# A hybrid encoder layer on one NeuronCore: side tasks placed by shared PSUM banks, a later hand-over of key tiles, a reordered last period and scan

## The chip, the core and the metric

The kernel runs on one core of one Trainium2 chip. The metric is the device time of one execution in microseconds (us). Engines are named as in the profile: PE is TensorE (PEld its weight loads), DVE is VectorE, ACT is ScalarE, POOL is GpSimd, SP is SyncE, which here issues the DMAs. Each engine runs its own instructions in order and waits on semaphores of the others.

## What is computed

One layer over 2048 tokens of 1024 features, all in float32:

```
hn   = rms_norm(h) ;  proj = hn @ w_in           # 4 head groups' q, k, v, gates; z; xbc; dt; memory q, gate
att  = window_attention(rotary(q), rotary(k), v, sink) * silu(g_attn)    # |q-k| <= 128, 16 heads, 4 key heads
xbc  = silu(depthwise_conv5(xbc))
y    = ssd_scan(forward) + ssd_scan(backward) + d_skip * xs              # chunks of 128, states of 128 x 64
ssd  = group_rmsnorm(y * silu(z))
xat  = softmax(q_mem . mk) . mv * silu(g_mem)    # 4 heads, 256 memory tokens
out  = rms_norm(h + concat[att, ssd, xat] @ w_out)
```

## The kernel before

Products that need accuracy are made of three float32r products each: operands are split into a high part (an ACT cast, line 174) and a low part (a DVE subtraction, line 175), and `split3` multiplies high by high, high by low and low by high. These projections write PSUM tiles named `pj`, of which there are three banks. All side work shares the five others: two banks `s` (scores, states), two banks `t` (transposes, sums), one bank `o` (outputs).

After a start that prepares the memory keys and values, the tokens are worked off in four periods of 512, c = 3, 2, 1, 0, from the last to the first. A period computes keys and values, then for each of four head groups g the heads' queries and gates (`heads`), convolution inputs (`conv`), `z_gate` and `mem_project`. In period 0 all eight `conv` stand ahead of the groups. Then `early` multiplies the finished attention and memory columns of the late blocks by half of w_out, and `out_block` does the rest for each of 16 blocks of 128 tokens.

Beside this main stream run side tasks, written as generators: window attention of one block (`attention`), `mem_attention`, the local part of the SSD (`ssd_local`), the decay sums (`steps`), and at the end the forward scan (`incoming` and `forward`, one block after the other). A task runs until a `yield`, whose number says after how many microseconds it may go on. That time is counted on `clock`, a plan of TensorE's work that `mm` and `tr` advance for every matmul written. `main` lets the due tasks write their next piece after every few projection matmuls. So the plan fixes TensorE's order. The other engines' orders come from the framework's scheduler, which works with its own estimates.

A piece is written when its own time has come. Whether the bank that it will write has been read out is not asked: TensorE then waits at that matmul, and everything behind it in TensorE's order waits too. In `attention` block 0 of a group loads the keys and values (`khh`, `kll`, `vg`) and waits 9.0. The three other blocks go on when the tiles stand in `kv`:

```
            kv["t"] = kst, vg
            yield 9.0
        yield from take("pm", 4)
        while "t" not in kv:
            yield 0.5
```

Queries go through `rope`, are stored to `q_d` and loaded again as `qs`, transposed in HBM (lines 472 and 473). `rope` uses the tiles `rt0` and `rt1`, one buffer each. In the scan, `forward` of one block loads `yy` from `y_d` (line 731), adds `inc` (736), multiplies by z (738), squares on ACT (739), adds on DVE (741), sums on TensorE (`t<-ones,b`), makes a factor, spreads it on TensorE (`t<-yo,ones`), multiplies four times (line 756) and stores to `mix_d` (758). `yy` has one buffer, so the load for the next block waits for that store.

Of the kernel before, what the change touches and what calls it, by code (L numbers as in the profile page):

```python
# [45 lines left out]
def layer(ctx: ExitStack, tc: tile.TileContext, a: dict):  # L46
# [38 lines left out]

    def bank(pl, name):
        return pl.tile([P, 512], F32, name=name)

# [120 lines left out]
    def rope(pa, pb, tab):  # L209

        n = tab.shape[-1]
        t, u = (misc.tile([P, 2, CH], F32, name=f"rt{i}")[:, :, :n] for i in range(2))
# [3 lines left out]
        hi = as32r(misc.tile([P, 2, CH], F32, name="rt1")[:, :, :n])  # L216
        split(hi, as32r(t), t)
        return hi, as32r(t)
# [161 lines left out]
    def steps(s, nb, raw):  # L380
# [21 lines left out]
        yield 18.0  # L402
        pf = bank(ps_t, "t")
# [5 lines left out]
        mm(pf[:, 256:256 + n], ones, raw.rearrange("p b r -> p (b r)"), True, True)  # L409
        fl = fc.rearrange("p b d r -> p (b d r)")  # L410
# [6 lines left out]
        yield 1.5  # L417
        pt = bank(ps_t, "t")
        nc.tensor.transpose(pt[:n, :P], fl, ident)
# [61 lines left out]
    def attention(c, g, i, qs, gt, kv):  # L481
# [7 lines left out]
        if i == 4 * c:  # L489
# [35 lines left out]
        yield 14.0 if c or g < 3 else 9.0  # L525
# [3 lines left out]
        for n_, j in enumerate(order):  # L529
            if n_ == 2:  # L530
                yield 0.7
            tt = bank(ps_t, "t")
            for r in range(4):
                tr(tt[:, r * P:(r + 1) * P], pm[:, r, j * P:(j + 1) * P])
            if n_ == 1:
# [4 lines left out]
        held["pm"] += 4  # L540
        oo = bank(ps_o, "o")
        for j in order:
            vv = vg[:, k0 + j - lo]
            mm(oo[0:64, 0:256], vv, pts[j][:, 0:256], j == order[0], j == order[-1])
            mm(oo[64:128, 0:256], vv, pts[j][:, 256:512], j == order[0], j == order[-1])
        held["pt"] += nk
# [32 lines left out]
    def ssd_local(blocks):  # L579
# [4 lines left out]
        for i, (c, g) in enumerate(parts):  # L584
# [4 lines left out]
            xc, ee = nxt  # L589
            tt = bank(ps_t, "t")  # L590
            for j in range(3):
                tr(tt[:, j * P:(j + 1) * P], xc[:, j])
            nat = sp.tile([P, 3 * P], F32, name="nat", bufs=1)
            nc.scalar.copy(nat, tt[:, :3 * P])  # L594
            pc = bank(ps_s, "s")
            mm(pc[:, :P], xc[:, 2], xc[:, 3], True, True)
            cbm = sp.tile([P, 2, P], F32, name="cbm")
# [14 lines left out]
            yield 14.0  # L612
            py = bank(ps_o, "o")
            for pr in range(2):
                for u in range(2):
                    r = 2 * pr + u
                    mm(py[u * 64:(u + 1) * 64, pr * P:(pr + 1) * P], nat[:, r * 64:(r + 1) * 64], gg[:, r], True, True)
            yo = sp.tile([P, 2, P], F32, name="yo")
# [3 lines left out]
            nc.sync.dma_start(y_d[2 * g:2 * g + 2, :, c * P:(c + 1) * P].rearrange("j p t -> p j t"), yo)  # L622
            pst = bank(ps_s, "s")
            mm(pst, nat[:, 256:384], xd.rearrange("p d r e -> p (d r e)"), True, True)
            so = sp.tile([P, 2, 256], F32, name="carry")
# [7 lines left out]
    def mem_project(c, xs, hd):  # L633
# [12 lines left out]
        return spawn("mem", mem_attention(c, hd, qh, ql, gm, mkt))  # L646

    def mem_attention(c, hd, qh, ql, gm, mkt):
        yield 11.0
        pms = []  # L650
        for half in range(2):
            ss = bank(ps_s, "s")
            for j in range(2):
                tl = slice((2 * half + j) * P, (2 * half + j + 1) * P)
                for _ in split3(ss[:, j * MEM:(j + 1) * MEM], [(qh[:, tl], ql[:, tl], mkt[:, :MEM], mkt[:, MEM:])]):
                    pass
            mx = misc.tile([P, 2], F32, name="mmx", bufs=3)
# [11 lines left out]
            if half:  # L669
                mvt = mkt.rearrange("p (u m d) -> p u m d", u=2, m=2)  # L670
                nc.sync.dma_start(as32(mvt), mv_d[:, :, :, hd * P:(hd + 1) * P].rearrange("u m p d -> p u m d"))
            yield 2.0 if half == 0 else 10.0
        yield from take("pt", 2)
        pts = []
        for m in range(2):
            tt = bank(ps_t, "t")
            for q in range(4):
                tr(tt[:, q * P:(q + 1) * P], pms[q // 2][:, q % 2, m * P:(m + 1) * P])
            hi = ap_.tile([P, 512], F32R, name="pt", bufs=3)
# [6 lines left out]
        yield 2.0  # L686
        oo = bank(ps_o, "o")
        for _ in split3(oo, [(mvt[:, 0, m], mvt[:, 1, m], pts[m][1], pts[m][2]) for m in range(2)]):
            pass
        held["pt"] += 2  # L690
# [3 lines left out]
    def incoming(c):  # L694
# [13 lines left out]
        yield 5.0  # L708
        for d, st_ in enumerate((state["f"], hbt)):
            py = bank(ps_s, "s")  # L710
            for pr in range(4):
                mm(py[:, pr * P:(pr + 1) * P], st_[:, pr * P:(pr + 1) * P], cc[:, pr // 2], True, True)
            nc.vector.tensor_tensor(ef[:, d], py.rearrange("p (q t) -> p q t", q=4), ef[:, d], ALU.mult)
            if d == 0:
                yield 1.0
# [7 lines left out]
    def forward(c):  # L723
# [18 lines left out]
        yield 15.0  # L742
        pn = bank(ps_t, "t")
        for g in range(2):
            mm(pn[:, g:g + 1], zv[:, g, 0], ones[:, 0:1], True, True)
        rn = sp.tile([P, 2], F32, name="rn", bufs=2)
# [118 lines left out]
    nz = [0] * NPER  # L865
    for c in range(NPER - 1, -1, -1):
# [3 lines left out]
        if c == 0:  # L870
            for i in range(8):
                main(conv(c, xs, i))
# [218 lines left out]
```

## Time and profile before

| | us |
|---|---|
| Median of three runs (lowest and highest) | 1881.1 (1878.04 to 1883.53) |
| The profiled execution | 1886.97 |
| its span, from first to last instruction | 1885.3 |
| PE busy in the span | 1770.2 |
| DVE busy, ACT busy, POOL busy | 1183.9, 925.1, 263.9 |

The profile shows one execution. Busy time of PE is a modelled one, since matmuls are pipelined. Idle time in front of an instruction stands in brackets in the timeline, with what ended it. PEclk is the granted clock of TensorE: 1.00 is 2.4 GHz and 0.50 is 1.2 GHz.

### The profile page before, as it was taken

What the parts mean: (1) busy time and instruction counts of PE and PEld (TensorE: products, weight loads), DVE (VectorE), ACT (ScalarE), POOL (GpSimd) and SP (SyncE); (2) the same over time, 40 slices, a digit from 0 to 9 for tenths busy, and PEclk for the clock granted to TensorE, in tenths of its full rate; (3) what the DMA queues carried; (4) which work ended last, traced back from release to release, by engine and by line L of the source; (5) the groups of instructions that cost most, each with busy time, mean ns of one, the idle gap of its engine ahead of it and who ended that gap; (6) DMA issues with size and microseconds to landing.
All of it is one profiled execution on the core that took longest, in us unless ns stands there. A gap on an engine that the chain in (4) does not pass through costs nothing.

```text
span 1885.3 us, 26616 instructions
## 1 busy us (share of the span) xinstructions
PE 1770.2 (94%) x9242; PEld 1441.6 (76%) x9242; DVE 1183.9 (63%) x2669; ACT 925.1 (49%) x1985; POOL 263.9 (14%) x253
## 2 busy tenths in 40 slices
PE   6789999998999999989999998999898989999998
PEld 6777878876778777866778787777676778888876
DVE  7456666686666668767576679866777543344332
ACT  6246546563756457456556665465566421111111
POOL 0000000012110000211000012211122233333220
PEclk9899999999999999999999999999999999999999
DMA  6746374577664755766474566655667765555442
GB/s 233 220 147 203 110 236 130 153 231 234 212 183 136 222 157 163 246 196 206 135 209 142 166 199 204 219 171 155 204 176 207 244 168 168 169 173 160 136 140 79
DMA packets 262695, 341.31 MB, mean 181 GB/s; under 512 B 29344, under 2 KB 171808, under 8 KB 262560
## 3 DMA queue, kind: packets, MB, share of 16 engines
q1 hardware_dynamic: 262560, 339.61, 59.2%
q8 instruction: 73, 1.20, 0.3%
q14 instruction: 62, 0.51, 0.1%
HBM read 251.20 MB, written 88.34 MB: 180 GB/s over the span
## 4 chain that ended last, share of the span: by engine, by line
PE 67%; DMA 14%; DVE 11%; ACT 4%; issue 3%; POOL 1%; SPq 1%; DVEq 0%; POOLq 0%; ACTq 0%
PE pj L156 50%; PE s L156 7%; PE o L156 5%; PE t L160 4%; DMA qs<-q_d 3%; DVE wl L175 2%; DMA q_d<-rt 2%; DMA cu<-in_x_dram 1%; DMA fb<-ef_d 1%; ACT wh L174 1%; DMA ws<-in_w_in_dram 1%; DMA mxl<-mix_d 1%; PE t L156 1%; DMA mix_d<-b 1%; DVE pm L512 1%
## 5 line engine op out<-in xcount | busy, mean ns | idle before, releaser
L156 PE MATMUL pj<-xh,wh 128*128 128x512 f32 (+2 forms) x1296 | 507.5, 392 | 1.6 <-ACT msq L852 1.6
L156 PE MATMUL pj<-xl,wh 128*128 128x512 f32 (+2 forms) x1296 | 495.9, 383 | 1.9 <-DVE xl L175 1.9
L156 PE MATMUL pj<-xh,wl 128*128 128x512 f32 (+2 forms) x1296 | 495.4, 382 | 0.1
L156 PEld LDWEIGHTS pj<-xh,wl 128*128 128x128 f32 x1296 | 247.5, 191 | 46.1 <-DVE wl L175 1.0
L156 PEld LDWEIGHTS pj<-xh,wh 128*128 128x128 f32 x1296 | 247.9, 191 | 40.9 <-issue 4.8
L156 PEld LDWEIGHTS pj<-xl,wh 128*128 128x128 f32 x1296 | 248.0, 191 | 36.8 <-DVE xl L175 2.4
L175 DVE TENSOR_TENSOR wl<-ws,wh 128x1024 fp32r<-128x1024 f32 (+2 forms) x175 | 211.4, 1209 | 96.1 <-ACT wh L174 89.5
L174 ACT CAST wh<-ws 128x1024 fp32r<-128x1024 f32 (+2 forms) x175 | 179.8, 1028 | 139.5 <-PE pj L156 96.9
L512 DVE CUSTOM_DVE_ANT_0 pm<-s,band,sink 128x384 f32<-128x384 f32 (+1 forms) x256 | 148.9, 594 | 68.6 <-PE s L156 66.9
L520 ACT ACTIVATE pm<-pm,mx 128x385 f32<-128x385 f32 (+1 forms) x256 | 151.2, 594 | 64.4 <-DVE mx L518 64.2
L608 POOL TENSOR_TENSOR b<-nat,win 128x256 f32<-128x256 f32 x64 | 44.3, 711 | 912.9 <-ACT nat L594 912.9
L156 PE MATMUL pj<-woh,mxh 128*128 128x512 f32 x416 | 171.4, 412 | 0.0
L156 PE MATMUL pj<-wol,mxh 128*128 128x512 f32 x416 | 166.1, 399 | 0.0
L156 PE MATMUL pj<-woh,mxl 128*128 128x512 f32 x416 | 166.1, 399 | 0.0
L156 PE MATMUL s<-khh,qs 128*128 128x384 f32 (+1 forms) x256 | 97.2, 380 | 55.0 <-DMA qs<-q_d 28.7
L524 ACT ACTIVATE pm<-pm,den 128x384 f32<-128x384 f32 (+1 forms) x256 | 132.9, 593 | 14.7 <-DVE den L522 14.7
L174 ACT CAST mxh<-mxl 128x512 fp32r<-128x512 f32 x64 | 39.6, 619 | 198.4 <-DMA mxl<-mix_d 94.9
L538 ACT COPY pt<-t 128x512 f32<-128x512 f32 x120 | 69.8, 582 | 103.7 <-PE t L160 103.5
L156 PEld LDWEIGHTS s<-khh,qs 128*128 128x128 f32 x256 | 50.3, 196 | 82.6 <-issue 35.1
L452 DVE SCALAR_TENSOR_TENSOR cu<-raw,cw,cu 128x512 f32<-128x512 f32 (+2 forms) x128 | 98.7, 778 | 15.6 <-ACT cu L450 14.5
L175 DVE TENSOR_TENSOR mxl<-mxl,mxh 128x512 fp32r<-128x512 f32 x64 | 50.4, 788 | 89.9 <-ACT mxh L174 89.8
L160 PE MATMUL t<-ident,pm 128*128 128x128 f32 x736 | 101.1, 274 | 2.7 <-ACT pt L538 1.8
(217 smaller groups left out, 2948.1 us busy)
## 6 DMA issues: line engine op xcount, KB each, us to landing
ws<-in_w_in_dram SPq DMA_DIRECT2D x152, 512.0 KB, 4.2
q_d<-rt SPq DMA_DIRECT2D x32, 512.0 KB, 5.5
qs<-q_d SPq DMA_DIRECT2D x32, 512.0 KB, 6.3
fb<-f_d SPq DMA_DIRECT2D x32, 512.0 KB, 4.6
mxl<-mix_d SPq DMA_DIRECT2D x64, 256.0 KB, 3.8
mix_d<-ao SPq DMA_DIRECT2D x64, 128.0 KB, 3.7
xc<-xbc_d SPq DMA_DIRECT2D x32, 256.0 KB, 3.8
st_d<-carry SPq DMA_DIRECT2D x32, 256.0 KB, 4.0
```

The lines of the kernel that those rows point to most:

```text
L156: nc.tensor.matmul(out, lhsT=lhsT, rhs=rhs, start=start, stop=stop)
L160: nc.tensor.transpose(out, in_, ident)
L174: nc.scalar.copy(hi, x)
L175: (eng or nc.vector).tensor_tensor(lo, x, as32(hi), ALU.subtract)
L452: nc.vector.scalar_tensor_tensor(u, raw[:, r0 + k:r0 + k + cnt], cw[:, i, k:k + 1], u, ALU.mult, ALU.add)
L512: nc.vector.tensor_tensor_reduce(pm[:, r, :w], ss[:, :w], band[:, ms], 1.0, sink8[:, 4 * g + r:4 * g + r + 1], ALU.add, ALU.max, mx[:, r:r ...
L520: nc.scalar.activation(pm[:, r, :w + 1], pm[:, r, :w + 1], AF.Exp, bias=mx[:, r:r + 1], scale=0.125, accum_out=den[:, r:r + 1])
L524: nc.scalar.activation(pm[:, r, :w], pm[:, r, :w], AF.Copy, scale=den[:, r:r + 1])
L538: nc.scalar.copy(pts[j], tt)
L608: nc.gpsimd.tensor_tensor(xd[:, d], nat[:, 0:256].rearrange("p (r e) -> p r e", r=4), win[:, d, 4 * g:4 * g + 4].unsqueeze(2).broadcast_to ...
```

## The change

Five edits. (1) `bank` notes for the shared banks until when each is taken, `slot` makes a task wait until the next bank of its kind is free by the plan's clock, and `reads` sets that time behind the last matmul into it: now plus 1.0 to 3.0. Every side task calls them, and some fixed waits change. (2) The key tiles are handed over after the wait, which is 10 instead of 9. (3) `mvt`, the memory values, has a tile of its own and is loaded by `mem_project`, not into the keys' tile later. (4) `rope` uses the four `xp` buffers where its pieces are small. (5) The last period spreads `conv` and `z_gate` over its groups, the waits of the scan are shorter and longer in places, and `early` may go on until the scan's second block is done.

```diff
+    turn = {"s": 0, "t": 0, "o": 0}
+    until = {"s": [0.0] * 2, "t": [0.0] * 2, "o": [0.0]}
+
     def bank(pl, name):
+        if name in turn:
+            until[name][turn[name] % len(until[name])] = clock[0] + 3.0
+            turn[name] += 1
         return pl.tile([P, 512], F32, name=name)
+
+    def slot(name, n=1):
+        while True:
+            u = until[name]
+            t = max(u[(turn[name] + i) % len(u)] for i in range(n))
+            if t <= clock[0]:
+                return
+            yield max(t - clock[0], 0.1)
+
+    def reads(name, us, back=1):
+        u = until[name]
+        u[(turn[name] - back) % len(u)] = clock[0] + us
...
     def rope(pa, pb, tab):
+        small = 2 * n <= XW
+        def half(name):
+            if small:
+                return misc.tile([P, XW], F32, name="xp", bufs=4)[:, :2 * n].rearrange("p (j t) -> p j t", j=2)
+            return misc.tile([P, 2, CH], F32, name=name)[:, :, :n]
...
     def attention(c, g, i, qs, gt, kv):
+            yield 10.0
             kv["t"] = kst, vg
-            yield 9.0
         yield from take("pm", 4)
...
         for r in range(4):
+            yield from slot("s")
             ss = bank(ps_s, "s")
             mm(ss[:, :w], qs[:, r, tl], kst[0][:, ks], True, False)
             mm(ss[:, :w], qs[:, r, tl], kst[1][:, ks], False, True)
+            reads("s", 1.7)
...
-                yield 1.2
+                yield 0.6
...
-        yield 14.0 if c or g < 3 else 9.0
+        yield 14.0 if c else 10.0
...
     def mem_project(c, xs, hd):
-        return spawn("mem", mem_attention(c, hd, qh, ql, gm, mkt))
+        mvt = misc.tile([P, 2, 2, P], F32R, name="mvt")
+        nc.sync.dma_start(as32(mvt), mv_d[:, :, :, hd * P:(hd + 1) * P].rearrange("u m p d -> p u m d"))
+        return spawn("mem", mem_attention(c, hd, qh, ql, gm, mkt, mvt))
...
     def incoming(c):
-        yield 5.0
+        yield 7.0
         for d, st_ in enumerate((state["f"], hbt)):
+            yield from slot("s")
             py = bank(ps_s, "s")
...
             if d == 0:
-                yield 1.0
+                yield 0.6
...
     def forward(c):
-        yield 15.0
+        yield 11.0
+        yield from slot("t")
         pn = bank(ps_t, "t")
...
-        yield 4.0
+        yield 5.5
+        yield from slot("t")
         pn = bank(ps_t, "t")
         mm(pn[:, :2 * P], ones, dg.rearrange("p g t -> p (g t)"), True, True)
+        reads("t", 2.0)
...
-        if c == 0:
-            for i in range(8):
-                main(conv(c, xs, i))
-            ssd_t = spawn("ssd", ssd_local(range(3, -1, -1)))
...
-            if c == 0 and g < 3:
+            if c == 0:
                 need(mem_t)
                 mem_t = main(mem_project(c, xs, g))
...
+            for i in range(2 * g, 2 * g + 2) if c else ((0, 1, 2, 3, 4), (5, 6, 7), (), ())[g]:
+                main(conv(c, xs, i))
+                if i == 7:
+                    ssd_t = spawn("ssd", ssd_local(range(4 * c + 3, 4 * c - 1, -1)))
+            for i in (g,) if c else ((), (0,), (1,), (2, 3))[g]:
+                main(z_gate(c, xs, i))
...
     rest_wo()
+    while last > 3 and not fwd[1].done:
+        main(early(last))
+        last -= 1
     for c in range(NB):
         main(out_block(c))
```

The matmuls are the same 8479 instructions in another order. On PE in the last period, where the first two blocks of head group 3 are written (`khh`, `kll`: keys, high and low; `qs`: queries; `mkt`: memory keys), there stood before:

```order
L156 MATMUL s<-khh,qs 128x256
L156 MATMUL s<-kll,qs 128x256
L156 MATMUL s<-khh,qs 128x256
L156 MATMUL s<-kll,qs 128x256
L156 MATMUL s<-mkt,qh 128x256 x2
L156 MATMUL s<-mkt,ql 128x256
L156 MATMUL s<-mkt,qh 128x256 x2
L156 MATMUL s<-mkt,ql 128x256
L156 MATMUL s<-khh,qs 128x256
L156 MATMUL s<-kll,qs 128x256
```

and for the same head group now, with projections in between:

```order
L177 MATMUL s<-khh,qs 128x256
L177 MATMUL s<-kll,qs 128x256
L177 MATMUL pj<-xh,wh 128x512
L177 MATMUL pj<-xl,wh 128x512
L177 MATMUL pj<-xh,wl 128x512
L177 MATMUL pj<-xh,wh 128x512
L177 MATMUL pj<-xl,wh 128x512
L177 MATMUL pj<-xh,wl 128x512
L177 MATMUL s<-khh,qs 128x256
L177 MATMUL s<-kll,qs 128x256
```

Four tiles that share two banks followed each other at once; now six projection matmuls stand between two of them.

On PE in the scan, around the sum `t<-ones,b` of one block (`s<-cbm`: what comes in from the states for the next block; `pj`: output products), before:

```order
L156 MATMUL pj<-woh_14708,mxl 128x512
L156 MATMUL pj<-woh_14714,mxh 128x512
L156 MATMUL pj<-wol_14713,mxh 128x512
L156 MATMUL pj<-woh_14714,mxl 128x512
L156 MATMUL t<-ones,b_15295 128x1 x2
L156 MATMUL pj<-woh_14319,mxh 128x512
L156 MATMUL pj<-wol_14318,mxh 128x512
```

and after:

```order
L177 MATMUL s<-cbm,state 128x128 x4
L177 MATMUL pj<-woh_14096,mxh 128x512
L177 MATMUL pj<-wol_14095,mxh 128x512
L177 MATMUL pj<-woh_14096,mxl 128x512
L177 MATMUL pj<-woh_14725,mxh 128x512
L177 MATMUL pj<-wol_14724,mxh 128x512
L177 MATMUL pj<-woh_14725,mxl 128x512
L177 MATMUL s<-cbm,b_15581 128x128 x4
L177 MATMUL t<-ones,b_15567 128x1 x2
```

The sum moved up to right behind the products with the states. From one block's `t<-yo,ones` to the next block's `t<-ones,b` there stood 66 `pj` matmuls, and 48 stand there now; from `t<-ones,b` to `t<-yo,ones` 24, and now 30.

On DVE at the first keys (`rt` or `xp`: rope; `wl`: low part of a weight), before:

```order
L175 TENSOR_TENSOR rt_629<-rt_629,rt_634 128x2x320
L507 COPY pm<-sink_133 128x4 x2
L175 TENSOR_TENSOR wl<-ws,wh 128x544
L214 TENSOR_TENSOR rt_667<-pj,tab 128x2x320
L213 TENSOR_TENSOR rt_666<-pj,tab 128x2x320
L215 TENSOR_TENSOR rt_666<-rt_666,rt_667 128x2x320
```

and after:

```order
L539 COPY pm<-sink_133 128x4 x2
L196 TENSOR_TENSOR xp<-xp 128x640
L241 TENSOR_TENSOR xp<-pj,tab 128x640
L242 TENSOR_TENSOR xp<-pj,tab 128x640
L196 TENSOR_TENSOR wl<-ws,wh 128x544
L243 TENSOR_TENSOR xp<-xp 128x640
```

The low part of the last value weights moved behind the two rope products that read PSUM.

## Rows read from the trace of the kernel before

**Rows 1.** The page's busy times: engine, busy us (share), instructions.

```profile
PE 1770.2 (94%) x9242; PEld 1441.6 (76%) x9242; DVE 1183.9 (63%) x2669; ACT 925.1 (49%) x1985; POOL 263.9 (14%) x253
```

**Rows 2.** Waits of PE, whole span: line, releaser, total us, times, longest.

```profile
PE s L156 <- DMA qs<-q_d: 28.7, 7, 7.5
PE s L156 <- DVE mx L512: 24.6, 17, 3.5
...
PE t L156 <- DVE b L741: 6.0, 1, 6.0
```

**Rows 3.** Busy times by stretch: stretch, length, PE PEld DVE ACT POOL, PEclk, DMA, GB/s.

```profile
110.00:1075.00 965.00, 918.14 (x4894) 743.06 (x4893) 650.46 (x1491) 562.50 (x1229) 67.93 (x68) 0.98 0.59 181
1075.00:1470.00 395.00, 366.68 (x2001) 294.38 (x2000) 302.08 (x737) 235.08 (x523) 78.49 (x71) 0.97 0.64 196
1470.00:1886.00 416.00, 399.18 (x1876) 327.71 (x1874) 164.48 (x331) 81.48 (x160) 110.21 (x100) 0.98 0.53 155
```

**Rows 4.** The same view, four stretches right behind waits for queries.

```profile
118.58:122.45 3.87, 3.87 (x14) 3.79 (x15) 1.65 (x6) 0.00 (x0) 0.00 (x0) 0.50 0.01 3
...
463.38:467.19 3.81, 3.81 (x10) 3.33 (x11) 1.25 (x4) 0.00 (x0) 0.00 (x0) 0.50 0.73 250
...
815.79:818.77 2.98, 2.98 (x8) 2.69 (x9) 1.25 (x4) 0.00 (x0) 0.00 (x0) 0.50 0.77 263
549.12:552.53 3.41, 3.41 (x14) 1.82 (x15) 0.19 (x2) 0.00 (x0) 0.24 (x1) 0.50 0.47 133
```

**Rows 5.** Timeline of PE, period 2's first scores: start, us, instruction, [idle before].

```profile
455.23 0.39 PE L156 MATMUL pj<-xl,wh 128*128 128x512 f32 x1
455.46 0.39 PE L156 MATMUL pj<-xh,wl 128*128 128x512 f32 x1
463.38 0.66 PE L156 MATMUL s<-khh,qs 128*128 128x384 f32 x1 [7.54 <-DMA qs<-q_d]
```

**Rows 6.** Timeline of PE and DVE around one wait for a score bank.

```profile
861.82 0.34 PE L156 MATMUL s<-khh,qs 128*128 128x384 f32 x1
...
863.88 2.15 DVE L575 SCALAR_TENSOR_TENSOR b<-fb,fc,b 128x128 f32<-128x128 f32 x3
...
867.21 0.69 PE L156 MATMUL s<-khh,qs 128*128 128x384 f32 x1 [3.48 <-DVE mx L512]
```

**Rows 7.** Timeline of all engines, one block of the scan.

```profile
1579.56 0.60 PE L156 MATMUL t<-yo,ones 128*128 128x256 f32 x2
...
1581.35 0.36 SPq L758 DMA_DIRECT2D mix_d<-b  x1
...
1583.66 0.38 SPq L731 DMA_DIRECT2D b<-y_d  x1
...
1586.62 1.28 POOL L736 TENSOR_TENSOR b<-b,fb 128x512 f32<-128x512 f32 x1 [5.72 <-DMA b<-y_d]
...
1590.30 0.58 DVE L741 TENSOR_TENSOR b<-b 128x256 f32<-128x256 f32 x1 [1.85 <-ACT b L739]
...
1597.09 0.50 PE L156 MATMUL t<-ones,b 128*128 128x1 f32 x4
```

**Rows 8.** The same, first, second and last of the scan's 15 links.

```profile
1476.26 0.59 PE L156 MATMUL t<-yo,ones 128*128 128x256 f32 x2
...
1492.99 0.41 DVE L741 TENSOR_TENSOR b<-b 128x256 f32<-128x256 f32 x1
...
1500.66 0.59 PE L156 MATMUL t<-yo,ones 128*128 128x256 f32 x2
...
1523.86 0.41 DVE L741 TENSOR_TENSOR b<-b 128x256 f32<-128x256 f32 x1
...
1819.39 0.67 PE L156 MATMUL t<-yo,ones 128*128 128x256 f32 x2
...
1832.09 0.42 DVE L741 TENSOR_TENSOR b<-b 128x256 f32<-128x256 f32 x1 [4.31 <-ACT b L739]
```

**Rows 9.** Timeline of DVE and PE at the first keys' rope.

```profile
66.56 0.72 DVE L175 TENSOR_TENSOR wl<-ws,wh 128x544 fp32r<-128x544 f32 x1
...
72.73 0.82 DVE L214 TENSOR_TENSOR rt<-pj,tab 128x640 f32<-128x640 f32 x1 [5.44 <-DMA k_d<-rt]
...
73.70 0.57 PE L156 MATMUL pj<-wh,xh 128*128 128x272 f32 x1 [5.25 <-DVE rt L214]
```

More of the change, by code (lines that the diff above doesn't have):

```diff
@@ L211, in rope @@
         n = tab.shape[-1]
-        t, u = (misc.tile([P, 2, CH], F32, name=f"rt{i}")[:, :, :n] for i in range(2))
+        small = 2 * n <= XW
[3 more added lines that the diff above has]
+            return misc.tile([P, 2, CH], F32, name=name)[:, :, :n]
+        t, u = half("rt0"), half("rt1")
         nc.vector.tensor_tensor(t, pa.unsqueeze(1).broadcast_to([P, 2, n]), tab[:, 1:3], ALU.mult)
@@ L215, in rope @@
         nc.vector.tensor_tensor(t, t, u, ALU.add)
-        hi = as32r(misc.tile([P, 2, CH], F32, name="rt1")[:, :, :n])
+        hi = as32r(half("rt1"))
         split(hi, as32r(t), t)
@@ L409, in steps @@
         mm(pf[:, 256:256 + n], ones, raw.rearrange("p b r -> p (b r)"), True, True)
+        reads("t", 1.6)
         fl = fc.rearrange("p b d r -> p (b d r)")
@@ L529, in attention @@
         for n_, j in enumerate(order):
-            if n_ == 2:
-                yield 0.7
+            yield from slot("t")
             tt = bank(ps_t, "t")
@@ L534, in attention @@
                 tr(tt[:, r * P:(r + 1) * P], pm[:, r, j * P:(j + 1) * P])
+            reads("t", 1.3)
             if n_ == 1:
@@ L540, in attention @@
         held["pm"] += 4
+        yield from slot("o")
         oo = bank(ps_o, "o")
@@ L545, in attention @@
             mm(oo[64:128, 0:256], vv, pts[j][:, 256:512], j == order[0], j == order[-1])
+        reads("o", 1.4)
         held["pt"] += nk
@@ L589, in ssd_local @@
             xc, ee = nxt
+            yield from slot("t")
             tt = bank(ps_t, "t")
@@ L612, in ssd_local @@
             yield 14.0
+            yield from slot("o")
             py = bank(ps_o, "o")
@@ L622, in ssd_local @@
             nc.sync.dma_start(y_d[2 * g:2 * g + 2, :, c * P:(c + 1) * P].rearrange("j p t -> p j t"), yo)
+            yield from slot("s")
             pst = bank(ps_s, "s")
             mm(pst, nat[:, 256:384], xd.rearrange("p d r e -> p (d r e)"), True, True)
+            reads("s", 1.4)
             so = sp.tile([P, 2, 256], F32, name="carry")
@@ L651, in mem_attention @@
         for half in range(2):
+            yield from slot("s")
             ss = bank(ps_s, "s")
@@ L656, in mem_attention @@
                     pass
+            reads("s", 3.0)
             mx = misc.tile([P, 2], F32, name="mmx", bufs=3)
@@ L674, in mem_attention @@
         pts = []
+        yield from slot("t", 2)
         for m in range(2):
@@ L685, in mem_attention @@
             pts[m] = tt, hi, lo
-        yield 2.0
+        yield 3.0
+        yield from slot("o")
         oo = bank(ps_o, "o")
@@ L689, in mem_attention @@
             pass
+        reads("o", 1.4)
         held["pt"] += 2
@@ L741, in forward @@
         nc.vector.tensor_tensor(zv[:, :, 0], zv[:, :, 0], zv[:, :, 1], ALU.add)
-        yield 15.0
+        yield 11.0
+        yield from slot("t")
         pn = bank(ps_t, "t")
@@ L745, in forward @@
             mm(pn[:, g:g + 1], zv[:, g, 0], ones[:, 0:1], True, True)
+        reads("t", 1.0)
         rn = sp.tile([P, 2], F32, name="rn", bufs=2)
@@ L889, in layer @@
                 norm_x(c - 1, rows_x(c - 1, dg))
-            if c:
-                main(conv(c, xs, 2 * g))
-                main(conv(c, xs, 2 * g + 1))
-                if g == 3:
-                    spawn("ssd", ssd_local(range(4 * c + 3, 4 * c - 1, -1)))
-            for _ in range(1 if c else ((1, 1, 1, 0))[g]):
-                main(z_gate(c, xs, nz[c]))
-                nz[c] += 1
+            for i in range(2 * g, 2 * g + 2) if c else ((0, 1, 2, 3, 4), (5, 6, 7), (), ())[g]:
[4 more added lines that the diff above has]
+                main(z_gate(c, xs, i))
             if c:
@@ L902, in layer @@
         if c == 0:
-            need(mem_t)
-            mem_t = main(mem_project(c, xs, 3))
-            for i in range(nz[c], NG):
-                main(z_gate(c, xs, i))
             fwd = [spawn("fwd", forward(b)) for b in range(NB)]
```

18 lines of the change are left out of this document (11 added, 7 removed).

## The prediction, made before the changed kernel was run

> **What bounds the kernel now.** First the busy times: PE is busy for 1770.2 of 1885.3 us, the next engine for 63% [rows 1]. The change moves matmuls and adds none, so the 1770 can only shrink where the clock was low; what can be won is PE's idle time and what a low clock costs behind it. Second, the waits of PE [rows 2]: 28.7 us in seven waits for the queries `qs`, 24.6 us in 17 waits for a score bank that DVE (line 512) has not read out, then single ones, of which the scan's 6.0 (line 741) matters here. Third, the stretches [rows 3]: PE idles 965 - 918.1 = 46.9 us in the periods 3 to 1, 28.3 in the last period with the attention that follows it, 16.8 in the scan and output stage. The first 110 us are a start that the change touches at one place only. Fourth, the clock: behind waits for queries PEclk reads 0.50, which is 1.2 GHz, in four stretches of 3.0 to 3.9 us [rows 4], though PE is busy there from end to end. A wait so costs more than its length.
>
> Matmuls of 512 columns follow each other at 0.23 us [rows 5]. With this and the like spacing of the smaller forms I count distances along both orders, as us of matmul work at full clock.
>
> **Queries due (edit 2).** In the old order the hand-over stood ahead of the wait of 9, so only block 0 waited; the blocks behind it wrote their scores at once. From the last matmul of the query projection to the first score stood 21.3 us of work in period 2, and PE still waited 7.54 us there [rows 5], so the queries took 28.8. Over the 16 groups the shortest distance was 17.7; it is 29.2 now, 30.8 at the place just named. Only one short wait, in the last period, meets a distance that hardly grew (34.9 before, 36.7 now). I let all 28.7 go; at most 3 come back. What the clock loses behind them goes too: half of 3.87 + 3.81 + 2.98 + 3.41 = 14.1 us, since busy time at 1.2 instead of 2.4 GHz counts double, so 7.0 [rows 4]. Term one: -36 (bounds -30 and -36). What comes late next? The attention of a group starts some ten us later, and its transposes and outputs with it; they have the next group's projections as cover, since the plan has work to put between until the end of the last period.
>
> **Bank read-outs (edit 1, and with it 3 and the last period of 5).** What is left of idle time between 110 and 1470 us is 46.9 + 28.3 - 28.7 = 46.5 [rows 2, 3]. The low clock costs (1 - 0.98) x 965 + (1 - 0.97) x 395 = 31 us there by the stretches' rounded clock [rows 3]; without the 7.0 of term one, and without the low clock that only met idle time, I put it at 20, an estimate. So 66 us are at stake. Which of it goes? Counted along the order, a shared bank (s, t, o) was taken again with under 1.5 us of matmul work behind its last matmul at 52 places, mostly in the last period; now at 17. Waits at such places go. But a wait like the one at 867 stays possible: the bank's matmul ran at 861.82, and its reader stood in DVE's queue behind 2.15 us of SSD work (line 575) and more, so the bank came free 5 us later [rows 6]. The note of 1.7 us knows nothing of that queue. I take 60% of the last period's share (28.3 idle and 9 of clock, -22) and a quarter of the other 30 (-8). Term two: -30, bounds 0 and -55.
>
> A rule of the Trainium skill speaks against it. Rows first: the score waits repeat all through, 17 of them, 24.6 us [rows 2]. "Perfetto Trace Analysis", section Identifying Performance Opportunities, says that the same gap repeating on the engine that should be saturated can mean that there isn't enough PSUM for the next tile, so a matter of buffer count. The change adds no bank. By that rule term two would be nothing; it is the first rival below. That the waits sat at close places in the order speaks for respacing, the queue at 867 for the rule.
>
> The early load of `mvt` puts one DMA at another place in SP's queue. It waits for the previous head's products, as the load of the keys beside it does already, so it adds no new block there. Cost nothing; if its cover failed, the weight loads behind it on SP would be late by the same wait, under 3 us a time, 16 times.
>
> **The start (edit 4).** DVE waited 5.44 us for the keys' store before line 214, and PE 5.25 behind it [rows 9]. That wait can go, since `xp` has four buffers. But the low part of the value weights (0.72 us), which ran at 66.56, now stands behind both rope products, and PE needs it for six matmuls before it reaches the place of the old wait. So the wait for the table of angles holds PE one step earlier. I take 0, bounds -4 and +2.
>
> **The scan (rest of edit 5).** Each block's chain is: `t<-yo,ones`, four products, a store to `mix_d`, the load of the next `yy` into the same buffer, two POOL operations, a square, line 741, then `t<-ones,b`. In the block shown, `t<-yo,ones` starts at 1579.56, the store is issued at 1581.35, the load at 1583.66, POOL starts at 1586.62, line 741 ends at 1590.88: 11.3 us. PE came to `t<-ones,b` at 1597.09, 17.5 us behind [rows 7], so 6 us of slack. Now 48 matmuls stand there, not 66: 17.5 - 18 x 0.23 = 13.4 us. Read the same way, the 15 links take 17.1 (the first), 23.6 (the second, which waits 6.0 today) to 13.1 (the last) [rows 2, 8], 14.4 on average, and eight lie above 13.4, by 26 us in sum. If nothing else changed, the stage would wait 26 instead of 6, and some low clock on top: +32 at most. But in four of the long ones line 741 stood in DVE's order behind two products (line 713) that waited for a DMA; in the new order those stand behind line 741, for they follow from matmuls right ahead of the sum. That takes some 3 us off each. I take +9, bounds -8 and +32. The other half of the loop grows from 24 to 30 matmuls, 1.4 us more for the factor, which is cover. At the end the last block's output begins 42 matmuls, 9.7 us, behind its last `t<-yo,ones`; store and load took 7 us in the block shown [rows 7] and the split follows: 0, bounds 0 and +3.
>
> **Sum.** Against the profiled execution, 1887.0 (its span and 1.7 around it): -36 - 30 + 0 + 9 = -57, so 1830. That execution lay 5.9 above the median of three runs, so 1824 on their scale.
>
> **Rivals.**
> The bank waits move and do not go. For it: DVE's queue [rows 6], and that the number of banks is the same. Against it: 52 close places and now 17. Then only terms one and the scan count: 1881.1 - 36 + 9 = 1854. Chance 0.20.
>
> The scan becomes the bound, slower than before. PE has to wait at each of the 15 sums, and each wait of 3 us and more drops the clock, which costs another 1.7 (half of the 3.41 us seen at 0.50 [rows 4]). It decides once it eats 66 us, 4.4 a link, that is from links of 13.4 + 2.7 = 16 us on average. Today they are 14.4, with links of 17.1 and 23.6 as witnesses, and the denser order puts more DMA traffic into each us. With 18.5 us: 5.1 + 1.7 = 6.8 a link, 102 in all, so 1881.1 - 66 + 102 - 6 = 1911. Against it: the plain chain is 11.3. Chance 0.08.
>
> The spacing does not do what it says: the plan's clock runs away from the chip, because TensorE's work takes longer than it books, and each respaced tile meets other queues on DVE. New waits as long as the old ones then eat term two and half of term one: 1881.1 - 18 + 15 = 1878. For it: DVE's and ACT's orders come from other estimates than the plan's. Against it: a plan that runs late only adds distance. Chance 0.07.
>
> All of the bank waits and the scan's go: 1881.1 - 36 - 55 - 8 = 1782. Chance 0.05.
>
> **The numbers.** My forecast, 1824, has 0.60, with its own range 1804 to 1848. The first rival widens the range to 1868, the good end to 1797. Three tenths of a per cent, 5.6 us, is about what a measurement of this kernel tells from no change. Faster than that: the forecast, the first rival, the good case and a little of the third, 0.86. Within: most of the third, 0.06. Slower: 0.08.
>
> **What would show it.** In the profile after: no row of waits for `qs` above 3 us in sum, and PEclk 1.00 where the four stretches stood; waits on line 512's successor around 15 us with longest ones of 2 to 4 us behind SSD work on DVE; in the last period's stretch idle time near 14 us; waits of `t<-ones,b` in the scan 10 to 20 us in sum, in short pieces. I am wrong in the main step if the score waits keep their 24 us, wrong in the scan's if they are gone or above 35.

## The result and the profile after

The changed kernel takes 1849.8 us (median of four runs, 1848.8 to 1855.0), 0.985 of the time before (0.982 to 0.988). The forecast, 1824, was 57 below the median of before; measured are some 28 by the ratio, 31 between the medians. The sign held, and the whole range (1797 to 1868) holds the result; the forecast's own range (1804 to 1848) just misses it, and the size is half of what was forecast. Profiled: 1848.8, span 1847.1, so 38.2 below the profiled execution of before, which lay high.

The page's busy times answer to [rows 1]:

```profile
PE 1755.7 (95%) x9242; PEld 1426.0 (77%) x9242; DVE 1179.9 (64%) x2681; ACT 921.4 (50%) x1985; POOL 260.3 (14%) x253
```

Waits of PE in the changed kernel (line, releaser, total us, times, longest), to be read against [rows 2]:

```profile
PE s L177 <- DVE mx L546: 14.7, 13, 6.8
...
PE pj L177 <- ACT mxh L195: 8.9, 1, 8.9
PE t L177 <- DVE b L792: 8.1, 7, 2.0
PE t L181 <- ACT nat L632: 6.7, 4, 4.7
...
PE s L177 <- ACT carry L670: 3.8, 1, 3.8
...
PE t L181 <- ACT pm L558: 2.4, 3, 1.1
```

No row for `qs` is left of 28.7 us. The score banks fell from 24.6 to 14.7. New are `mxh` (the high part of a block's finished columns), `nat` (transposed SSD inputs), `carry` (SSD states) and `pm` (softmax weights), 21.8 us together: casts, copies and scalings on ACT that PE hardly waited for before. The stretches, as in [rows 3]:

```profile
110.00:1075.00 965.00, 929.11 (x4986) 749.45 (x4986) 666.63 (x1522) 572.65 (x1251) 70.65 (x70) 0.99 0.61 186
1075.00:1470.00 395.00, 375.95 (x2046) 299.51 (x2045) 282.30 (x717) 231.52 (x520) 58.06 (x59) 0.98 0.63 194
1470.00:1848.00 378.00, 360.30 (x1709) 296.33 (x1707) 160.83 (x324) 68.97 (x138) 122.20 (x109) 0.99 0.60 177
```

PE idles 35.9 us in the first stretch (46.9 before), 19.0 in the second (28.3), 17.7 in the third (16.8). Over the span idle time fell from 115.1 to 91.4, and PE's busy time by 14.5.

Where do the new waits come from? The timeline of the changed kernel at three of them (start, us, engine, instruction, [idle before it]):

```profile
118.78 0.34 PE L177 MATMUL s<-khh,qs 128*128 128x384 f32 x1
...
122.73 1.28 ACT L610 ACTIVATE b<-fb,fc 128x128 f32<-128x128 f32 x4 [6.24 <-DMA fb<-f_d]
123.17 1.23 DVE L611 SCALAR_TENSOR_TENSOR b<-fb,fc,b 128x128 f32<-128x128 f32 x4 [5.74 <-ACT b L610]
...
127.49 0.61 DVE L546 CUSTOM_DVE_ANT_0 pm<-s,band,sink 128x384 f32<-128x384 f32 x1
...
128.17 0.69 PE L177 MATMUL s<-khh,qs 128*128 128x384 f32 x1 [6.76 <-DVE mx L546]
...
467.87 0.63 ACT L302 ACTIVATE cu<-cu 128x512 f32<-128x512 f32 x1 [8.29 <-DMA cu<-in_x_dram]
...
468.50 0.57 ACT L670 COPY carry<-s 128x512 f32<-128x512 f32 x1
...
469.11 0.69 PE L177 MATMUL s<-khh,qs 128*128 128x384 f32 x1 [3.82 <-ACT carry L670]
...
1394.14 0.38 PE L177 MATMUL s<-xc 128*128 128x128 f32 x2
...
1402.71 1.30 ACT L195 CAST mxh<-mxl 128x512 fp32r<-128x512 f32 x2 [7.69 <-DMA mxl<-mix_d]
1403.38 0.79 PE L177 MATMUL pj<-wh,mxh 128*128 128x512 f32 x1 [8.86 <-ACT mxh L195]
```

At 128 the score of 118.78 is read at 127.49, since DVE stood before an SSD operation (line 611) which needs a load through ACT. At 469 the bank's copy stood on ACT behind a square (line 302) which waited 8.3 us for a load of `x`. At 1403 the first `early` block's own columns arrive late. All three end at an operation on DVE or ACT that stands behind a DMA: the first two are late readers of a bank, the third makes an operand. Two stand within 10 us of where the waits for queries at 118 and 463 stood.

### The profile page after: what moved, and what is told of

Same layout as the page of the kernel before. It is cut to its first block, busy times and chain, and to the rows that moved or that the text cites. A ratio compares the mean times of both kernels' runs of the same rounds, so it can differ in the third digit from the quotient of the medians.

```text
span 1847.1 us, 26627 instructions
## 1 busy us (share of the span) xinstructions
PE 1755.7 (95%) x9242; PEld 1426.0 (77%) x9242; DVE 1179.9 (64%) x2681; ACT 921.4 (50%) x1985; POOL 260.3 (14%) x253
## 5 line engine op out<-in xcount | busy, mean ns | idle before, releaser
L177 PEld LDWEIGHTS pj<-xh,wl 128*128 128x128 f32 x1296 | 246.0, 190 | 46.9 <-DVE wl L196 2.7
L195 ACT CAST mxh<-mxl 128x512 fp32r<-128x512 f32 x64 | 39.5, 617 | 162.8 <-DMA mxl<-mix_d 105.7
L181 PEld LDWEIGHTS t<-ident,pm 128*128 128x128 f32 x736 | 86.5, 142 | 34.6 <-ACT nat L632 7.6
L177 PE MATMUL o<-pt,vg 128*64 128x256 f32 x736 | 93.8, 388 | 1.6 <-DVE dq L425 0.7
```

Source lines behind the costliest of these rows:

```text
L177: nc.tensor.matmul(out, lhsT=lhsT, rhs=rhs, start=start, stop=stop)
L181: nc.tensor.transpose(out, in_, ident)
L195: nc.scalar.copy(hi, x)
```

## The experiments

All ratios are against the kernel before on the same chip, with their 95% interval; the changed kernel's is 0.985.

**One edit alone, and all but one.** `e1_handover` is the kernel before with edit 2, `e7_banks` before with edits 1 and 3, `e8_bank_hand` before with all three. `e2_noslot` and `e6_oldhand` are the changed kernel without edit 1, and without edit 2.

```diff
# e1, in the kernel before; e6 is the reverse, in the changed kernel
+            yield 10.0
             kv["t"] = kst, vg
-            yield 9.0
# e2, with the fixed waits of before put back
     def slot(name, n=1):
-        while True:
+        return
+        yield
```

> The kernel before with edit 2 alone (the key tiles are handed over after a wait of 10). The forecast's term one as it stands: all seven waits for queries (28.7 us) and 7.0 of low clock go, 0.981 of before, 1845. Theory after the traces, that a wait removed on TensorE comes back in part as a wait for a bank whose reader is queued behind other work: in the changed kernel 6.8 us stand at 128 and 3.8 at 469, near where 6.9 and 7.5 stood; so some 20 to 24 of the 36 remain, 0.988, 1858. In the profile: no row for queries, the row of score banks longer than the 24.6 us of before.

> The changed kernel with `slot` returning at once and the fixed waits of before between scores, transposes and outputs (1.2, 0.7, 2.0, 1.5, 1.0): edit 1 alone undone. Forecast's term two: most of 30 us come back, 1875, waits for score banks near 24 us again. Theory that the spacing won next to nothing because the waits moved into the queues of the reading engines: within 8 us of the changed kernel, 1842 to 1858, and the total idle time of TensorE within 10 us of the changed kernel's 91.

> The changed kernel with edit 2 undone: the key tiles are handed over ahead of the wait of 9, as before. Forecast's term one: the waits for queries come back, 28.7 us and 7 of low clock, so 36 above the changed kernel, 1886. Theory after the first four runs, in which edit 2 alone took all waits for queries away and the total idle time of TensorE stayed (115 before, 118), so that the time was only passed on to banks and their readers: with the spacing in place the hand-over is worth less, 10 to 20, so 1860 to 1870. Rival: it is worth nothing here either, 1850.

> The kernel before with edits 1 and 3 alone (spacing by banks, own tile for the memory values). Forecast's term two with little of the last period's part: -15 to -30, 1851 to 1866. Theory after the first runs (taking the spacing out of the changed kernel cost 45): the spacing carries the gain, -25 to -45 by itself, 1836 to 1857, the waits for queries staying at 20 to 29 us. Rival: the spacing only pays for the bursts that the later hand-over makes, so that by itself it is worth nothing, 1881.

> The kernel before with edits 1, 2 and 3, last period, scan and rope as before. Sum of the forecast's terms one and two without the last period's share: -36 - 8 to -36 - 30, 1815 to 1837. Theory: 1850 to 1865, since undoing the last period's order alone cost 15 (1864) and the rest of the change is worth little without it. If the two edits were additive as found apart (hand-over alone +15), it is 15 above the run with the spacing alone.

| | ratio | us |
|---|---|---|
| e1: edit 2 alone | 1.008 (1.005 to 1.011) | 1898.0 |
| e7: edits 1, 3 alone | 1.014 (1.011 to 1.017) | 1904.3 |
| e8: edits 1, 2, 3 | 0.991 (0.989 to 0.993) | 1861.6 |
| e2: changed, without edit 1 | 1.006 (1.004 to 1.009) | 1895.5 |
| e6: changed, without edit 2 | 1.012 (1.010 to 1.015) | 1902.5 |

Each edit alone makes the kernel slower, by 15 and 26 us; both together make it faster, by 17. Given the rest of the change, they are worth 51 (edit 2, by e6) and 40 (edit 1, by e2). I had not expected this: only e8 lies where a theory put it. Waits of PE with edit 2 alone:

```profile
PE s L156 <- DVE mx L512: 25.7, 26, 2.9
PE t L160 <- ACT nat L594: 11.1, 4, 4.9
...
PE pj L156 <- DVE xl L175: 7.8, 7, 1.7
PE s L156 <- ACT mpm L663: 7.7, 7, 4.3
PE t L160 <- DVE pt L536: 5.8, 5, 3.1
```

The waits for queries are gone, as forecast, and PE idles 1892.9 - 1775.3 = 117.6 us, 2.5 more than before. The idle time came back in full, at banks whose readers are late: ACT and DVE now get scores, transposes and SSD copies in the same few microseconds. Of the 15 us by which this kernel is slower, the profiled executions show only 7.6 (2.5 idle, 5.1 busy); the rest is not accounted for. One place of it, in the same run:

```profile
858.36 2.13 ACT L524 ACTIVATE pm<-pm,den 128x384 f32<-128x384 f32 x4
860.38 0.57 ACT L626 COPY carry<-s 128x512 f32<-128x512 f32 x1
860.85 0.48 ACT L594 COPY nat<-t 128x384 f32<-128x384 f32 x1
...
861.38 0.90 PE L160 MATMUL t<-ident,pm 128*128 128x128 f32 x3 [4.30 <-ACT nat L594]
```

`nat` frees a `t` bank, and stands on ACT behind four softmax scalings. With the spacing alone:

```profile
PE s L177 <- DMA qs<-q_d: 39.5, 8, 9.6
PE pj L177 <- ACT mxh L195: 14.1, 3, 9.5
PE s L177 <- DVE mx L546: 10.4, 12, 2.6
```

The spacing does what it says, 24.6 to 10.4 at the score banks, but the waits for queries grow from 28.7 to 39.5, and the scan's first sum comes at 1508.6 instead of 1471.4. Why they grow was not traced.

**The last period and the scan.** `e3_oldlast` is the changed kernel with the old last period (eight `conv` first, memory head 3 and two `z_gate` last); `e4_oldscan` with the scan's old waits and without the rule on `early`; `e9_oldwaits` with the old waits alone.

```diff
# e3
+        if c == 0:
+            for i in range(8):
+                main(conv(c, xs, i))
...
-            for i in (g,) if c else ((), (0,), (1,), (2, 3))[g]:
-                main(z_gate(c, xs, i))
+            for _ in range(1 if c else ((1, 1, 1, 0))[g]):
+                main(z_gate(c, xs, nz[c]))
# e9 and e4 (in incoming 5.0 and 1.0)
-        yield 11.0
+        yield 15.0
         yield from slot("t")
...
-        yield 5.5
+        yield 4.0
         yield from slot("t")
# e4 alone
-    while last > 3 and not fwd[1].done:
-        main(early(last))
-        last -= 1
```

> The changed kernel with the order of the last period of before (eight conv ahead of the groups, memory head 3 and two z gates at the end, wait 9 in the last attention): that part of edit 5 undone. If the new order's one wait of 8.9 us at 1403 (output columns loaded late, with 10 us of low clock around it) is all that it brings, undoing it gains 8.9 + 5 and gives back some of the nine short waits of before between 1320 and 1470 (20 us with their share of clock): 1845 to 1856, no difference that can be told. Rival, the forecast: the last period's order with the spacing is worth 22, so 1872.

> The changed kernel with the scan's waits of before (15, 4, 5, 1) and without the rule that `early` goes on: the scan part of edit 5 undone. Forecast: the change cost 9, so 1841 (0.979). Theory from the traces: idle time of the stage is the same (16.8 before, 17.7 now) and low clock fell from 17 to 5 us there, so undoing it costs up to 6: 1850 to 1856.

> The changed kernel with the scan's waits of before (15, 4, 5, 1), but with the rule that `early` goes on until the scan's second block is done. It tells apart the two halves of the scan edit, which together are worth 76 us (1925.6 without them). If the rule carries it, because four blocks instead of eight had their first half multiplied early and the last blocks' work then no longer covers a link of the scan: 1845 to 1860, with 8 or more blocks early. If the waits carry it (a link planned as 19 plus what the banks add, instead of 16.5): above 1895, with waits for `mxh` of 20 us and more.

Measured: e3 0.990 (0.988 to 0.993), e4 1.022 (1.019 to 1.025), e9 1.013 (1.011 to 1.016). e3 and e4 lie outside everything that was expected; e9 lies where the second theory put it, that the waits carry the edit. e3 equals e8 (0.991) within the intervals: with the old last period, the new scan and rope bring nothing that can be told. With the new last period the scan's edit is worth 54 us (its waits alone, e9) to 70 us (with the rule on `early`, e4), not -9. The tail of e9:

```profile
1818.81 0.38 SPq L813 DMA_DIRECT2D mix_d<-b  x1
...
1821.56 1.05 SPq L988 DMA_DIRECT2D mxl<-mix_d  x2
...
1825.83 1.35 ACT L195 CAST mxh<-mxl 128x512 fp32r<-128x512 f32 x2 [10.83 <-DMA mxl<-mix_d]
...
1826.50 0.79 PE L177 MATMUL pj<-woh,mxh 128*128 128x512 f32 x1 [9.89 <-ACT mxh L195]
```

PE has no output product left but that of the block which the scan has just finished, and waits for its store, load and split. In e9 that happens in the last links only: 37.9 of its 47.8 us of waits for `mxh` stand behind 1785. In e4, with four blocks early, 28.1 of 65.0 us stand in the first links, from 1502 to 1686, where the rule on `early` gives PE other work.

**Three repairs.** `f1_ownx` loads the squares' input into `xp` instead of `cu`; `f2_fill` puts 9 us of side work ahead of the first `early`; `f4_both` does both; `f3_reads` has longer notes.

```diff
# f1
-                xn = misc.tile([P, XW], F32, name="cu", bufs=3)[:, :CH]
+                xn = misc.tile([P, XW], F32, name="xp", bufs=4)[:, :CH]
# f2, in early(c)
+        if c == NB - 1:
+            idle(clock[0] + 9.0)
# f3, in attention; the notes of 1.3 in ssd_local too
-            reads("s", 1.7)
+            reads("s", 2.7)
-            reads("t", 1.3)
+            reads("t", 2.3)
```

> The changed kernel with one buffer name changed: the squares that make the next period's row sums (line 302) are loaded into the `xp` buffers, not into the three `cu` buffers that the convolution holds. Theory that a wait on TensorE now ends at a reading engine that itself stands behind a late load: the first of these loads was issued only at 462.9 and ACT stood before line 302 for 8.3 us with the copy of a score bank behind it; loaded earlier, the waits at 469 (3.8, `carry`), and those from 492 to 499 (1.1, 1.1 and 4.7, `pm` and `nat`) shrink by 6 to 10 us, with 3 to 5 of low clock: 1835 to 1842 (0.976 to 0.980). Rival, that the bank distances alone set those waits: no change, 0.985, the waits stay at their places.

> The changed kernel with 9 us of side work put ahead of the first `early` block in TensorE's order, since its loads come 8.9 us late (into memory that the last projection weights held). If that wait is the new order's own price and side work is at hand: 4 to 9 us less and up to 5 of low clock, 1836 to 1846 (0.976 to 0.982). Rival: the side tasks wait for their own banks there, and the idle time stays in pieces: 1850.

> The changed kernel with longer notes: a score bank counted as taken for 2.7 us instead of 1.7, a transpose bank for 2.3 instead of 1.3. If the waits that are left come from readers that are a little late, they shrink by half: 14.7 us of score waits to 7, 1840 (0.980). If they come from readers that stand for 4 to 8 us in their engine's queue, a us more helps little: score waits above 11 us, time within 6 of the changed kernel. The changed order may also cost as edits 1 and 2 did apart: above 1860.

> Both edits of the two runs before (loads of the row sums into `xp`, side work ahead of the first `early` block). If the two waits are independent, the gains add: 1822 to 1838 (0.968 to 0.978), the best of all. If edits to the plan do not add, as edits 1 and 2 did not: no better than the better of the two.

f1: 0.981 (0.977 to 0.984), 1844.7, just above the 1835 to 1842 expected. The waits at 469 and from 492 to 499 are gone; a wait of 2.5 for `qs` stands at 465, and one of 1.8 for `carry` in period 3. Period 2, in the changed kernel and then in f1:

```profile
455.00:810.00 355.00, 338.68 (x1785) 268.04 (x1784) 248.61 (x577) 209.65 (x456) 34.23 (x33) 0.99 0.63 194
455.00:810.00 355.00, 344.05 (x1817) 272.98 (x1817) 256.85 (x600) 212.38 (x460) 37.34 (x37) 1.00 0.65 200
```

So a late load on a reader's engine set these waits, not the distance of banks. The gain in time, some 8 us, lies at the edge of what the intervals tell apart; the same edit brings some 7 between f2 and f4 and some 5 between g1 and g3 below, each within the intervals but all the same way. f2: 0.991 (0.988 to 0.994), 11 us slower than the changed kernel, which neither expectation allowed for: the wait for `mxh` went, and waits for `b` (10.2), `woh` (3.1) and shorter ones took its place; idle time stayed (93.1, where the changed kernel has 91.4). f4: 0.987 (0.984 to 0.990), not better than f1, as its second expectation had it. f3: 1.021 (1.018 to 1.025), in its last expectation (above 1860). Its score waits are 16.3, so a longer distance does not shorten what is left of them; and it waits 57.5 us for `mxh`, 49.3 of them behind 1750, as e9 does.

**What ends the scan.** My first idea was the number of blocks done early (12 in f3, 8 in the changed kernel, 2 before). `g2_early12` does twelve early in the changed kernel, `g1_cap8` is f3 with eight, `g3_best` the same with f1's buffers.

```diff
# g2
-    while last > 3 and not fwd[1].done:
+    while last > 3:
# g1, g3
-        if last < 4:
+        if last < 8:
...
-    while last > 3 and not fwd[1].done:
+    while last > 7 and not fwd[1].done:
```

> The changed kernel with twelve blocks early instead of eight, nothing else moved ahead of the scan's third block. Theory of cover: a block done early leaves 48 matmuls to the scan, another 96. Eight early leave 1152, or 14.8 links of 78 for the scan's 15; twelve leave 960, or 12.3 links: the last two or three links have nothing to cover them, with waits of 8 to 9 us for `mxh` and half clock: 50 to 80 us more, 1900 to 1930. Rival: matmuls done early are done, the sum is the same, so 1850 plus at most 10.

> The kernel with longer notes (2.7 for scores, 2.3 for transposes; 1921.8, twelve early blocks) with at most eight blocks early. Theory of cover: the loss of 72 against the changed kernel was the scan's end alone, so it is back at 1840 to 1856, with no wait for `mxh` above 5 us after 1700. Rival: the longer notes themselves delay the attention until the last period stalls: above 1880.

> As the run before, with the row sums' loads in the `xp` buffers too. If the waits at the start of period 2 and the score waits shrink independently: 5 below the better of the two, 1832 to 1845 (0.974 to 0.981), the fastest. If a plan's edits do not add: 1845 to 1860.

Measured: g2 0.993 (0.990 to 0.995), g1 1.024 (1.019 to 1.028), g3 1.021 (1.017 to 1.024). g1 lies where its rival put it, g2 and g3 where nothing did. The idea fell: the cap cures nothing, and twelve cost 15 us by the ratios, not 50 to 80. What the traces have in common is another number, the output products (`pj`) that stand behind the scan's first sum, since only these lie beside its links. It is read from the stretch from that sum to the end, for `pj` alone (columns as in [rows 3], the count of PE is what matters); in the changed kernel, with the same stretch for all tiles and two links below it:

```profile
1489.00:1848.00 359.00, 312.73 (x1290) 240.14 (x1290) 27.48 (x40) 0.00 (x0) 0.99 0.59 173
1489.00:1848.00 359.00, 341.41 (x1610) 280.56 (x1610) 150.74 (x313) 63.16 (x131) 111.22 (x102) 0.99 0.59 173
...
1598.90:1619.60 20.70, 18.95 (x78) 14.50 (x78) 1.38 (x2) 0.00 (x0) 1.00 0.60 161
1619.60:1640.40 20.80, 18.91 (x78) 14.51 (x78) 1.38 (x2) 0.00 (x0) 1.00 0.60 170
```

1290 products at 78 a link cover 16.5 links; the scan has 15, and the last block's output follows. The same stretch in f3:

```profile
1529.05:1921.00 391.95, 285.62 (x1110) 216.24 (x1110) 26.81 (x39) 0.00 (x0) 0.90 0.51 151
```

The first sum comes 40 us later and 1110 are left, 14.2 links. What that does at the end is seen link by link in e9 (`pj` alone, from sum to sum, its last four links):

```profile
1759.58:1784.70 25.12, 22.09 (x90) 16.59 (x90) 3.21 (x5) 0.00 (x0) 1.00 0.62 188
1784.70:1813.30 28.60, 16.79 (x61) 12.28 (x60) 1.38 (x2) 0.00 (x0) 0.82 0.48 130
1813.30:1842.94 29.64, 14.96 (x49) 10.65 (x48) 1.38 (x2) 0.00 (x0) 0.71 0.35 101
1842.94:1869.28 26.34, 13.48 (x49) 10.41 (x48) 1.38 (x2) 0.00 (x0) 0.74 0.29 90
```

Three links have not their 90 products but what is left and the 48 of the block just finished, and take 26 to 30 us at a lower clock. In f3 the last four are like this (60, 48, 48 and 48 products), in h5 below the last one (66); in the changed kernel the last link still has 84.

Two runs were made by this number, counted along their order before they ran: `h1_notes_early` (f1, longer notes in the attention of periods 3 to 1) and `h5_notes_last` (changed kernel, longer notes in that of the last period).

```diff
# h1; h5 has "if not c"; the transposes' notes are 2.3 or 1.3
-            reads("s", 1.7)
+            reads("s", 2.7 if c else 1.7)
```

> The changed kernel with the row sums' loads in the `xp` buffers and the longer notes (2.7 and 2.3) in the attention of the periods 3 to 1 only. Along its order 1296 output matmuls stand behind the scan's first sum, 16.6 links of 78. Theory of cover: the notes cost nothing in these periods, the scan's end is covered, idle time there 9 to 15 us: 1836 to 1850 (0.976 to 0.983). Rival, that longer notes slow the periods themselves: above 1870.

> The changed kernel with the longer notes in the attention of the last period only. Along its order 1206 output matmuls stand behind the scan's first sum, 15.5 links of 78, between the two groups seen so far. Theory of cover: one link or two bare at the end, 10 to 25 us more idle time with its half clock, 1860 to 1880 (0.990 to 1.000). Rival, that the periods' notes and not the cover make the loss: within 6 of the changed kernel, 1844 to 1856; or all of the loss of 72 is the last period's: 1920.

h1: 0.979 (0.975 to 0.982), 1842.4, the fastest of all. h5: 0.9985 (0.996 to 1.001), 1879.3. Both times lie where the theory of cover put them, and h5's idle time does (21.5 above the changed kernel's); h1's, 16.8, is above the 9 to 15 expected. Their stretches from the first sum on, h1 and then h5:

```profile
1482.00:1841.00 359.00, 314.66 (x1297) 241.20 (x1296) 27.28 (x40) 0.00 (x0) 1.00 0.60 175
```

```profile
1503.60:1871.00 367.40, 300.26 (x1206) 228.91 (x1206) 26.80 (x39) 0.00 (x0) 0.95 0.56 165
```

Idle is the stretch less all of PE's busy time in it:

| | products left | per link | links covered | idle, us | ratio |
|---|---|---|---|---|---|
| before | 1500 | 90 | 16.7 | 16.8 | 1 |
| h1 | 1296 | 78 | 16.6 | 16.8 | 0.979 |
| changed kernel | 1290 | 78 | 16.5 | 17.6 | 0.985 |
| g2 | 1290 | 78 | 16.5 | 26.8 | 0.993 |
| e8 | 1434 | 90 | 15.9 | 13.7 | 0.991 |
| h5 | 1206 | 78 | 15.5 | 39.1 | 0.9985 |
| e4 | 1296 | 90 | 14.4 | 72.7 | 1.022 |
| e9 | 1284 | 90 | 14.3 | 60.3 | 1.013 |
| f3 | 1110 | 78 | 14.2 | 75.0 | 1.021 |

The new order of the last period leaves 1290 products where 1500 were left. With 90 a link this covers 14.3, so the shorter waits of the scan are what keeps the changed kernel from a bare tail. Of e4's 72.7, part is the wait in its first links.

The eleven kernels that the table leaves out fit it: g1 and g3 cover 14.2 links and idle for 78 us there, the nine others cover 15.9 or more (e7 15.9, e6 16.2) and idle for 16 to 26. But cover isn't all: e1, e2, e6 and e7 are slower than the kernel before with such a covered scan, so what they lose stands ahead of it.

**The start.** `e5_oldrope` undoes edit 4.

```diff
-        small = 2 * n <= XW
+        small = False
```

> The changed kernel with edit 4 undone (`rope` on `rt0` and `rt1` at the start too). Forecast: the edit is worth 0 (-4 to +2), so 1850. Theory from the traces, in which the changed kernel has 30 more matmuls behind it at 110 us: the edit is worth 4 to 7, so 1854 to 1857 (0.987 to 0.989), with a wait of 5 us of TensorE for `rt` near 74.

0.987 (0.983 to 0.991), 1856.0. Its first 110 us, and then those of the changed kernel:

```profile
0.00:110.00 110.00, 85.55 (x474) 75.80 (x475) 66.70 (x112) 46.11 (x74) 7.26 (x14) 0.92 0.69 222
```

```profile
0.00:110.00 110.00, 90.32 (x508) 80.69 (x509) 70.17 (x120) 48.22 (x79) 9.35 (x15) 0.95 0.69 223
```

The edit takes 4.8 us of idle time out of the start. In the total that is within the intervals.

## Why the forecast had the sign and not the size

**What bounds the kernel** was right: PE's busy time fell by no more than the clock gave. By the mean granted clock (0.972 before, 0.985 now) I estimate (1 - 0.972) x 1885 - (1 - 0.985) x 1847 = 25 us; it fell by 14.5. The other ten stay open.

**Term one (-36)** failed at one step: "I let all 28.7 go; at most 3 come back." The first half is right; 0 of 28.7 is left. The second half is wrong sixfold. I asked what comes late next, and answered with PE's own cover, the next group's projections. The readers of the banks were the answer: alone, the edit gave back all it took (idle 115.1 to 117.6). In the changed kernel 17.5 us stand again at 128, 469 and 492 to 499, so a net gain of some 11 of idle time. These waits come with edit 2: e8 has 14.6 us of them at the same places, and e6, without edit 2, waits for queries at 116 and 459 instead. The clock's share came back in part too: from 118 to 133 PEclk reads 0.69, where it read 0.85.

**Term two (-30)**: the score waits came out as I put them in sum (15 expected, 14.7 measured), though the longest is 6.8 and not 2 to 4. The step that failed is "Which of it goes?": I took shares of idle time by counting distances between uses of one bank. Idle time between 110 and 1470 us, without the queries, went from 46.5 up to 54.9, since `mxh` at 1403 and the ACT copies are not on that count; the last period's stretch has 19.0 of it, not the 14 forecast. The queue at 867 [rows 6] showed the mechanism, and I priced it as a remainder.

**The sum** failed as a form. Terms one and two were added; measured, they are +15 and +26 apart and -17 together (forecast without the last period's share: -44), and given all the rest -51 and -40. So neither has a value of its own that could stand in a sum. The rest, last period, scan and start, adds another -11, close to the forecast's -22 + 9 by luck: with the scan's old waits the new last period loses (e9, 1.013, against 0.991 for e8).

**The scan (+9)** as a term: the waits at the sum are 8.1, below the 10 to 20 forecast, because the chains, read as in [rows 7], take 11.0 to 15.4 us in the denser order and 13.0 on average, not 14.4. What I missed is outside the term: that the number per link is also a budget, to be set against the products left.

**The start (0)** was 5 too careful; the low part's late turn (PE waits 3.06 for it at 70.8, and PEclk stays at 1.00 behind it) cost less than the wait for the store (5.25 at 73.7, with 0.50 in front of it and behind it). The second rival priced a wait of this length with a drop of the clock, which did not come here.

**The rivals.** The result lies near the first one's number, 1854, whose chance I gave as 0.20, but by luck: that number has term one in full and term two at nothing, where the queries brought a net 11 of 28.7 and edit 1, taken out, costs 40. What happened is nearer to the third's mechanism (0.07, respaced tiles that meet other queues), more on ACT than on DVE, at a smaller price. f1 shows that one group of waits was set by a load in front of the reader, and f3 that the score waits did not shrink with distance. The Trainium skill's rule beside the first rival ("Perfetto Trace Analysis", section Identifying Performance Opportunities) is that the same gap repeating on the engine that should be saturated can mean that there is not enough SBUF or PSUM for the next tile. For PSUM it is neither borne out nor refuted, since no run had another bank; on the side of SBUF f1 agrees with it, where a load with other buffers took away 10.8 us of waits at 469 and 492 to 499. The scan as the bound (0.08) did not come in the changed kernel. It came in five kernels that undo or stretch one piece of it, at 1904 to 1926, but not as I gave it: they wait for `mxh` in a few links, 48 to 65 us in all, and not at each of the 15 sums (7.0 us there at most), so that my 1911 lies among them is luck.

## What to carry to other kernels

When a wait on the busiest engine is taken away, follow the next resource to the engine that frees it, and ask what that engine stands behind: a load there can return the time. Edits to one order need not add, and here they did not; before adding two terms, run each alone and both. For a serial chain beside a stock of work, divide the stock that is left when the chain starts by the work planned per link: below the number of links the tail is bare, and a change far upstream, which merely starts the chain later, can cost more than it wins.

## What was not expected of the hardware

Nothing of the engines' own speed. A wait for the `mxh` of a finished block, store, load and cast, was 8.2 to 9.9 us at the end of e9, with nothing of PE's to lay beside it; three bare links and the last block's output cost e9 60.3 - 17.6 = 43 us more idle time than the changed kernel has there, and a granted clock of 0.93 instead of 0.99 over that stretch.
